# A second z unit behind the first, three groups in a row, and VectorE's half of the first rounding: a Mamba-2 and differential-attention trunk in fp32

## The chip, the cores and the metric

The kernel runs on one core of one Trainium2 chip. The metric is the device time of one execution in microseconds. The matrix unit (TensorE, PE in the profile, with its weight loads shown apart as PEld), VectorE (DVE), ScalarE (ACT), GpSimd (POOL) and SyncE (SP, which here only issues DMAs) each work through a queue of their own in order, and wait for each other by semaphores.

## What is computed

Two layers over 512 tokens of width 1024, all in float32. The first is a Mamba-2 layer, the second a differential attention layer against one shared set of keys and values; a norm ends it. The change touches the first layer alone:

```python
def mamba2_layer(x, norm_g, w_in, conv_w, conv_b, dt_bias, a_log, d_skip, gate_norm_g, w_out):
    h = rms_norm(x, norm_g)
    zxbcdt = h @ w_in                                  # z 2048 | x 2048, B 1024, C 1024 | dt 32
    z = zxbcdt[..., :SSM_D_INNER]
    xbc = silu(causal_depthwise_conv(zxbcdt[..., 2048:6144], conv_w, conv_b))   # 4 taps
    dt = softplus(zxbcdt[..., 6144:] + dt_bias)
    y = ssd_chunked_scan(xs * dt[..., None], -exp(a_log) * dt, bm, cm) + d_skip * xs
    y = gated_group_rms_norm(y, z, gate_norm_g)        # y * silu(z), normed in 8 groups of 256
    return x + y @ w_out
```

There are 8 groups of 4 heads; a group has its own B and C (128 wide each) and 256 columns of x.

## The kernel before

Each float32 product is made of three: both factors are split into a rounded half (`hi`) and a remainder (`lo`), and `mm3` issues hi by hi, hi by lo and lo by hi as 128x512 products. For a weight ScalarE makes `whi` from `raw`, with the norm's gain in it, and VectorE makes `wlo`; for the input the halves are `a_hi` and `a_lo` (`hh` and `hl` in the code, `split_x`).

The first layer is a row of units, `order_a`. A unit `z`*j* makes 512 columns of z (96 products of 128x512 in four banks `pz`, then Silu on ScalarE into `zs`, in halves of 256; group g needs `zt[g]`, so z*j* is for groups 2j and 2j+1). A unit `g`*i* makes B, C and x of one group (96 products in four banks `pg`), each bank followed by the convolution: VectorE multiplies the bank by the norm's row (`pg<-pg,ar_row`), ScalarE does the last tap and the bias (`xc<-pg`), VectorE the other three taps (`xc`, three instructions), ScalarE the Silu. A unit `o`*j* is a quarter of the output projection (`po`). Each unit fetches two blocks of weights, of 1 MB each, two blocks ahead (`segs`, `use`, `fetch`), through two `raw` buffers and three of `whi` and `wlo`. `TURNS` says in which order a unit takes its banks and its two blocks: kind 0 takes one block for all four banks and then the other, kind 1 both blocks for each of the first two banks.

Between these products the scan of each group (`ssd`) is fed in, piece by piece. A piece's place is in `PLACES`: so many blocks of three products after the group's own unit. `cb` makes C by B in a bank `pcb`; `bt` and `xt` transpose B and x (`pbt`, `pxt`), after which VectorE makes `xdt` and `dx`, POOL `xe`, and VectorE multiplies the decays `dec` by `pcb`; `st` makes the states (`psA`, `psB`, `hst`) and the products within a chunk (`pyd`, one half in a `long` bank); `o1` and `o2` make the parts from the states (`po1`, `po2`), VectorE scales them (`tmp`), POOL adds them, VectorE multiplies by z (`dx<-dx,zs`), ScalarE squares and sums, and VectorE makes the root of the norm in ten small steps (`v`, `y_i`, `y_y`, `y_c`); ScalarE scales by it (`tmp<-dx,y_y`); `y0` transposes the result (`pyt`), from which `yh` and `yl` are made for the output projection. There is one `long` bank; it holds `pcb` of a group, then half of `pyd`.

Ahead of all this stand z0 (its first block straight as the input lands), the norm of the input (`scales`: the root on VectorE, a diagonal `adiag`, and a product that spreads it over the partitions, `aps_r`), and the chain from `ps_dt` to the decays: about twenty instructions on VectorE, a transposition `ps_tt` at the place `tt`, a round trip through memory (`acs_d`, then `dec`), and per group eight POOL instructions and one exponential.

TensorE follows the program's order (`T.on`), so the table of places fixes its queue. VectorE's and ScalarE's queues in this layer are set by the scheduler of the tile framework, which puts weight halves ahead (`high_priority`) and fits the rest around them. Rows of the profile carry L70 where an engine is called through the helper `Ordered`.

Of the kernel before, what the change touches and what calls it, by code (L numbers as in the profile page):

```python
# [9 lines left out]
F32 = mybir.dt.float32  # L10
# [3 lines left out]
ALU = mybir.AluOpType  # L14
# [3 lines left out]
P = 128  # L18
S = 512
D = 1024  # L20
NT = S // P
# [16 lines left out]


PLACES = {  # L40
# [7 lines left out]
    "y2": (None,) * 7 + (72,),  # L48
}

# [28 lines left out]
def trunk(ctx, tc, x, x_t, par, w_dt, w_in, w_out, w_kvqg, w_bo, d_skip, lam_qk, fin_g, out):  # L79
    nc = tc.nc  # L80
    V, A, T = (Ordered(tc, e) for e in (nc.vector, nc.scalar, nc.tensor))
    GP = nc.gpsimd
# [4 lines left out]
    small = ctx.enter_context(tc.tile_pool(name="small", bufs=2))  # L87
# [13 lines left out]
    def long_bank(name):  # L101
        return psum.tile([P, 512], F32, tag="long", name=name)
# [1 line left out]

    order_a = "z0 g0 g1 z1 g2 g3 z2 g4 o0 g5 z3 g6 g7 o1 o2 o3".split()
    segs = []
    for it in order_a + ORDER_B:
        segs += [(it[0], int(it[1]) if len(it) == 2 else it, k) for k in range(2 if it[0] in "zgov" else 1)]  # L110
# [3 lines left out]
    nc.scalar.dma_start(prm[:], par[:, 0:C_CB])  # L114
    prc = const.tile([P, N_PAR - C_CB], F32, name="prc")
    x_tok = res.tile([P, NT, D], F32, name="x_tok")
    ident = const.tile([P, P], F32, name="ident")
    make_identity(nc, ident)
    sg1 = const.tile([P, 1], F32, name="sg1")
# [147 lines left out]
    def rsqrt(v, n, tag, bufs=2):  # L267


        y = small.tile([P, n], F32, tag=f"{tag}_y", name=f"{tag}_y", bufs=bufs)  # L270
        c = small.tile([P, n], F32, tag=f"{tag}_c", name=f"{tag}_c", bufs=bufs)
        iy = small.tile([P, n], I32, tag=f"{tag}_i", name=f"{tag}_i", bufs=bufs)

        def vyy():
            if n == 1:
                V.scalar_tensor_tensor(out=c, in0=y, scalar=v, in1=y, op0=ALU.mult, op1=ALU.mult)
            else:
                V.tensor_tensor(out=c, in0=y, in1=v, op=ALU.mult)
                V.tensor_tensor(out=c, in0=c, in1=y, op=ALU.mult)

        V.tensor_scalar(out=iy, in0=v.bitcast(I32), scalar1=1, scalar2=None, op0=ALU.logical_shift_right)
        V.tensor_scalar(out=y.bitcast(I32), in0=iy, scalar1=-1.0, scalar2=float(0x5F3759DF - 2 ** 31), op0=ALU.mult, op1=ALU.add)
        vyy()
        V.scalar_tensor_tensor(out=c, in0=c, scalar=-10.0 / 3.0, in1=c, op0=ALU.add, op1=ALU.mult)
        V.scalar_tensor_tensor(out=y, in0=c, scalar=5.0, in1=y, op0=ALU.add, op1=ALU.mult)
        vyy()
        root_end[0] = V.scalar_tensor_tensor(out=y, in0=c, scalar=-64.0 / 3.0, in1=y, op0=ALU.add, op1=ALU.mult)
        return y
# [39 lines left out]
    def scales(tag, ss):  # L328

        V.tensor_scalar(out=ss, in0=ss, scalar1=ROOT2 / D, scalar2=ROOT2 * EPS, op0=ALU.mult, op1=ALU.add)  # L330
        col = const.tile([P, NT], F32, tag="r_col", name=f"{tag}r_col")
        V.tensor_copy(col, rsqrt(ss, NT, "y"))
        w = small.tile([P, NT + 1, P], F32, tag="wide", name=f"{tag}diag", bufs=2)
        GP.memset(w[:, NT], 1.0)
        for t in range(NT):
            GP.tensor_tensor(out=w[:, t], in0=ident, in1=col[:, t:t + 1].to_broadcast([P, P]), op=ALU.mult)
        ps = long_bank(f"{tag}ps_r")
        T.on = True
        T.matmul(ps, lhsT=w[:, NT], rhs=w[:, 0:NT].rearrange("p t n -> p (t n)"), start=True, stop=True)
        T.on = False  # L340
        row = res.tile([P, S], F32, tag="r_row", name=f"{tag}r_row")
        A.copy(row, ps)
        return col, row
# [14 lines left out]
    def new_h(tag):  # L358
        return [res.tile([P, KD, S], F32R, tag=f"hT_{i}", name=f"{tag}_{i}") for i in ("hi", "lo")]
# [9 lines left out]
    hh, hl = new_h("a")  # L369
# [4 lines left out]
    bp2 = bctx.enter_context(tc.tile_pool(name="bp2", bufs=2))  # L374

    zt = {}
    yT = {}
    conv_out = {}

    def z_out(j, t, ps):  # L380

        for i in range(2):
            zs = bp2.tile([P, 256], F32, tag="zs", name=f"zs{j}_{t}_{i}", bufs=12)
            A.activation(zs, ps[:, i * 256:(i + 1) * 256], AF.Silu, scale=r_col[:, t:t + 1])
            zt[2 * j + i, t] = zs

    warm = ss_bank("warm")
    for i in range(17):  # L390
        T.transpose(warm[:, 0:P], ident, ident)
    xt = [bp2.tile([P, 2, S], F32, tag="yl", name=f"xt{i}", bufs=4) for i in range(4)]

    def split_x(k, n=slice(0, S)):
        A.copy(hh[:, k, n], xt[k // 2][:, k % 2, n])
        V.tensor_tensor(out=hl[:, k, n], in0=xt[k // 2][:, k % 2, n], in1=hh[:, k, n].bitcast(F32), op=ALU.subtract)


# [4 lines left out]
    wh, wl = ready.pop(("z", 0, 0))  # L403
    pz0 = [mm_bank(f"pz0_{t}") for t in range(NT)]
    V.on = A.on = True
    for k in range(4):
        lay(first[k])
        for n in (slice(0, 256), slice(256, S)) if k < 2 else (slice(0, S),):
            split_x(k, n)
    V.on = A.on = False  # L410
    for k in range(4):
        for t in range(NT):
# [2 lines left out]
    for k in range(4, KD):  # L415
        split_x(k)
# [3 lines left out]
    ss = bss[:, 1]  # L420
# [13 lines left out]
    for k in range(KD):  # L434
        for c in range(NQ):
            T.matmul(ps_dt[c * H:(c + 1) * H, 0:P], lhsT=dtw_raw[:, k, :], rhs=xt[k // 2][:, k % 2, c * P:(c + 1) * P],
                     start=k == 0, stop=k == KD - 1)
# [49 lines left out]
    def turned():  # L487
        yield "tt"
        ps_tt = ss_bank("ps_tt")
        for i, src in enumerate((dtp, acs, toe)):  # L490
            T.transpose(ps_tt[:, i * P:(i + 1) * P], src, ident)
        V.tensor_copy(tok[:, 0:3].rearrange("p a c h -> p (a c h)"), ps_tt[:, 0:3 * P])
        A.activation(tok[:, 3], tok[:, 1], AF.Exp)
        decays((0, 1))

    def runs_of(kind=1):

        at = {}
        for i, b, n in TURNS[kind]:
            k = at.get((i, b), 0)  # L500
            at[i, b] = k + n
            yield i, b, range(k, k + n)

    def z_proj(j):
        pz, w = {}, {}
        for t, b, ks in runs_of():
            if b not in w:
                w[b] = use(("z", j, b))
            if t not in pz:
                pz[t] = mm_bank(f"pz{j}_{t}")  # L510
            yield from tok_mm(pz[t], t, b, w[b], ks)
            if b and ks[-1] == 3:
                z_out(j, t, pz[t])
# [17 lines left out]
    def group_proj(g):  # L531
        fts = [(16 + g, "b", 1), (24 + g, "c", 2), (2 * g, "x0", 1), (2 * g + 1, "x1", 1)]
        pg, w, outs = {}, {}, []
        for i, b, ks in runs_of(min(g, 1)):
            if b not in w:
                w[b] = use(("g", g, b))
            if i not in pg:
                pg[i] = mm_bank(f"pg{g}_{i}")
            wh, wl = w[b]
            cs = slice(i * P, (i + 1) * P)  # L540
            for k in ks:
                kk = 4 * b + k
                mm3(pg[i], (wh[:, k, cs], wl[:, k, cs]), (hh[:, kk, :], hl[:, kk, :]), kk == 0, kk == KD - 1)
                yield
            if b and ks[-1] == 3:
                outs.append(conv(pg[i], *fts[i]))
        conv_out[g] = outs
# [26 lines left out]
    def resume(n, at, gen, places):  # L574
        kind = next(gen, None)
        if kind is not None:
            due.append((at + places[kind], len(due), at, gen, places))
# [19 lines left out]
    decs = {}  # L597
# [20 lines left out]
    def ssd(g):  # L618
        bc, cc, x0, x1 = conv_out.pop(g)
        xc = (x0, x1)  # L620
        dec, een, _ = decs.pop(g)
        hs = slice(R * g, R * g + R)

        yield "cb"
# [8 lines left out]
        bt = bp.tile([P, 3, P], F32, tag="bt", name=f"bt{g}")  # L633
# [4 lines left out]
        for j in range(2):  # L638
# [6 lines left out]
            with tc.issue_after(next_b.ins) if next_b else ExitStack():  # L645
                V.tensor_tensor(out=xdt[:, :, 2 * j:2 * j + 2, :], in0=pv, in1=dt_tok[:, :, h2].unsqueeze(3).to_broadcast([P, NQ, 2, HD]), op=ALU.mult)
                V.tensor_tensor(out=dx[:, :, 2 * j:2 * j + 2, :], in0=pv,
                                in1=dsk[:, h2].unsqueeze(1).unsqueeze(3).to_broadcast([P, NQ, 2, HD]), op=ALU.mult)
        xe = bp.tile([P, 3, R, HD], F32, tag="xe", name=f"xe{g}")
        for c in range(3):  # L650
            GP.tensor_tensor(out=xe[:, c], in0=xdt[:, c], in1=toe_tok[:, c, hs].unsqueeze(2).to_broadcast([P, R, HD]), op=ALU.mult)  # L651
        for h in range(R):
            V.tensor_tensor(out=dec[:, h], in0=dec[:, h], in1=pcb.rearrange("p (c l) -> p c l", l=P), op=ALU.mult)

# [36 lines left out]
        for c in (2, 3):  # L691
            T.matmul(po2[:, (c - 2) * 256:(c - 1) * 256], lhsT=cc[:, c * P:(c + 1) * P], rhs=hsf[:, c - 1], start=True, stop=True)
        V.tensor_tensor(out=tmp[:, 1], in0=po1[:, 256:512].rearrange("p (h e) -> p h e", e=HD),
                        in1=eacs_tok[:, 1, hs].unsqueeze(2).to_broadcast([P, R, HD]), op=ALU.mult)
        V.tensor_tensor(out=tmp[:, 2:4], in0=po2.rearrange("p (c h e) -> p c h e", h=R, e=HD),
                        in1=eacs_tok[:, 2:4, hs].unsqueeze(3).to_broadcast([P, 2, R, HD]), op=ALU.mult)
# [15 lines left out]
        yh = bp2.tile([P, 2, S], F32R, tag="yh", name=f"yh{g}", bufs=4)  # L712
# [3 lines left out]
        n = 2 if g == G - 1 else NQ  # L716
# [8 lines left out]
        yT[g] = (yh, yl)  # L725

    T.on = True
    resume(0, 0, turned(), {"tt": 22})
    first_layer()
    T.on = False  # L730

    hh, hl = new_h("b")
# [126 lines left out]
    st = {}  # L859
# [283 lines left out]
    y, f, o, dst = half(3, 0)  # L1143
# [8 lines left out]
    y, f, o, dst = half(3, 1)  # L1152
# [68 lines left out]
```

## Time and profile before

| | |
|---|---|
| median of 3 runs | 706.07 us (706.02 to 706.21) |
| the profiled execution | 707.18 us, of which 705.4 us span |
| PE busy | 696.1 us, 3838 matmul rows |
| DVE busy | 524.2 us |
| ACT busy | 426.3 us |
| POOL busy | 116.1 us |
| granted TensorE clock, mean | 0.998 |

The span goes from the first to the last instruction; the rest of an execution's time lies around it. A row of the chain or of a timeline begins with the start in us from the span's start and the length in us; xN counts merged instructions. What stands in square brackets is the idle time before it on its engine and what ended that. A row of the waits has the total in us, the count, and the longest. A plain float32 product shows as two rows, a transposition as one.

### The profile page before, as it was taken

To read this page: it belongs to the slowest core of one execution; us is meant where nothing else is said; L and a number is where in the kernel's file an instruction comes from. 1 tells how busy PE (TensorE), PEld (TensorE's weight loads), DVE (VectorE), ACT (ScalarE), POOL (GpSimd) and SP (SyncE) were. 2 spreads that over 40 slices of the span, in tenths; PEclk is the share of its full clock that TensorE was granted. 3 is DMA by queue.
4 is the path that set the end of the run, shared out by engine and by line. 5 is a ranking of instruction groups with operands and counts; after the bars stand their busy time and mean duration, and the time that the engine had idled before them with its cause. 6 is when DMAs were issued, how large, how long until landed. Compare 5 with 4: busy or idle time off the path is not lost.

```text
span 705.4 us, 10468 instructions
## 1 busy us (share of the span) xinstructions
PE 696.1 (99%) x3838; PEld 580.7 (82%) x3838; DVE 524.2 (74%) x1181; ACT 426.3 (60%) x931; POOL 116.1 (16%) x158
## 2 busy tenths in 40 slices
PE   8999999999999999999999999999999999999996
PEld 7888788888878888888888888888888888888884
DVE  5499967799489679569995757557778757787776
ACT  6859663573654547536635258567777667665546
POOL 0008242502406025042110101000000000000002
PEclk9999999999999999999999999999999999999999
DMA  8654314214125323313222111513112221130103
GB/s 293 257 193 170 120 60 135 105 61 179 42 79 180 105 76 120 110 70 120 64 84 94 60 60 53 194 60 113 67 60 77 80 83 61 60 106 14 31 1 119
DMA packets 13491, 70.85 MB, mean 100 GB/s; under 512 B 1792, under 2 KB 3328, under 8 KB 6016
## 3 DMA queue, kind: packets, MB, share of 16 engines
q1 hardware_dynamic: 13008, 69.90, 27.6%
q8 instruction: 30, 0.49, 0.3%
q10 hardware_dynamic: 432, 0.28, 0.1%
q14 instruction: 21, 0.17, 0.1%
HBM read 68.02 MB, written 2.16 MB: 99 GB/s over the span
## 4 chain that ended last, share of the span: by engine, by line
PE 78%; DVE 8%; ACT 5%; DMA 4%; issue 3%; POOL 2%; SPq 0%; ACTq 0%; POOLq 0%; DVEq 0%
PE po L70 16%; PE pg L70 14%; PE pt L70 8%; PE pq L70 6%; PE pk L70 6%; PE pv L70 6%; PE pz L70 6%; PE pb L70 3%; DMA raw<-in_w_in 3%; PE sc L70 3%; DVE wlo L70 2%; ACT whi L70 2%; PE pc L70 2%; PE pyd L70 2%; DVE xc L70 1%
## 5 line engine op out<-in xcount | busy, mean ns | idle before, releaser
L70 DVE SCALAR_TENSOR_TENSOR wlo<-raw,prm,whi 128x512 fp32r<-128x512 f32 (+1 forms) x240 | 149.3, 672 | 54.0 <-ACT whi L70 53.7
L70 ACT ACTIVATE whi<-raw,prm 128x512 fp32r<-128x512 f32 (+1 forms) x240 | 133.2, 629 | 46.7 <-PE pg L70 12.0
L70 PE MATMUL pg<-a_hi,whi 128*128 128x512 f32 x256 | 102.8, 402 | 0.0
L70 PE MATMUL pg<-a_hi,wlo 128*128 128x512 f32 x256 | 99.9, 390 | 0.0
L70 PE MATMUL pg<-a_lo,whi 128*128 128x512 f32 x256 | 99.7, 389 | 0.0
L70 DVE SCALAR_TENSOR_TENSOR xc<-pg,prc,xc 128x511 f32<-128x511 f32 (+2 forms) x96 | 70.9, 743 | 12.3 <-ACT xc L70 11.2
L70 PEld LDWEIGHTS pg<-a_hi,wlo 128*128 128x128 f32 x256 | 48.1, 188 | 10.3
L70 PEld LDWEIGHTS pg<-a_hi,whi 128*128 128x128 f32 x256 | 48.2, 188 | 9.6 <-ACT zs L70 0.2
L70 PEld LDWEIGHTS pg<-a_lo,whi 128*128 128x128 f32 x256 | 48.1, 188 | 9.4
L70 PE MATMUL po<-whi,yh 128*128 128x512 f32 x128 | 51.2, 400 | 0.0
L70 PE MATMUL pz<-whi,a_hi 128*128 128x512 f32 x128 | 49.7, 397 | 0.3 <-ACT a_hi L70 0.3
L70 PE MATMUL po<-whi,yl 128*128 128x512 f32 x128 | 49.9, 390 | 0.0
L70 PE MATMUL po<-wlo,yh 128*128 128x512 f32 x128 | 49.9, 390 | 0.0
L70 PE MATMUL pz<-whi,a_lo 128*128 128x512 f32 x128 | 48.9, 390 | 0.0
L70 PE MATMUL pz<-wlo,a_hi 128*128 128x512 f32 x128 | 48.9, 389 | 0.0
L1026 POOL TENSOR_TENSOR ot<-x_tok,fg 128x512 f32<-128x512 f32 x4 | 5.0, 1284 | 246.8 <-DVE x_tok L70 246.8
L70 ACT ACTIVATE xc<-xc 128x512 f32<-128x512 f32 x32 | 20.2, 630 | 40.5 <-DVE xc L70 36.7
L70 ACT ACTIVATE xc<-pg,prc 128x512 f32<-128x512 f32 x32 | 24.8, 774 | 28.3 <-DVE pg L70 27.9
L70 DVE CUSTOM_DVE_ANT_0 s<-sc,bias 128x128 f32<-128x128 f32 (+3 forms) x64 | 29.4, 488 | 16.0 <-PE sc L70 15.5
L70 ACT ACTIVATE s<-s,mx 128x128 f32<-128x128 f32 (+3 forms) x64 | 35.6, 557 | 9.1 <-DVE mx L70 8.9
L651 POOL TENSOR_TENSOR xe<-xdt,tok 128x256 f32<-128x256 f32 x24 | 14.0, 613 | 159.3 <-DVE xdt L70 159.3
L70 ACT ACTIVATE tmp<-dx 128x256 f32<-128x256 f32 x32 | 13.1, 410 | 36.8 <-DVE dx L70 36.8
(237 smaller groups left out, 1651.1 us busy)
## 6 DMA issues: line engine op xcount, KB each, us to landing
raw<-in_w_in SPq DMA_DIRECT2D x22, 1024.0 KB, 4.9
raw<-in_w_kvqg SPq DMA_DIRECT2D x16, 1024.0 KB, 4.8
dec<-acs_d SPq DMA_DIRECT2D x8, 1024.0 KB, 5.1
raw<-in_w_out SPq DMA_DIRECT2D x8, 1024.0 KB, 4.9
raw<-in_w_bo SPq DMA_DIRECT2D x4, 1024.0 KB, 4.8
x_tok<-in_x SPq DMA_DIRECT2D x4, 512.0 KB, 9.0
out<-ot SPq DMA_DIRECT2D x6, 256.0 KB, 2.1
raw<-in_w_in SPq DMA_DIRECT2D x4, 256.0 KB, 4.9
```

Source lines behind the costliest of these rows:

```text
L70: i = op(*args, **kw)
L651: GP.tensor_tensor(out=xe[:, c], in0=xdt[:, c], in1=toe_tok[:, c, hs].unsqueeze(2).to_broadcast([P, R, HD]), op=ALU.mult)
L1026: GP.tensor_tensor(out=o, in0=y, in1=f, op=ALU.mult)
```

## The change

- `order_a` becomes z0 z1 g0 g1 g2 z2 g3 g4 ... where it was z0 g0 g1 z1 g2 g3 z2 g4 ...; from g4 on the units are the same. `PLACES` has new numbers for groups 0 to 3 (and small ones for the last `y0`), and `tt` moves from 22 to 36. z1 now takes the first kind of turns, and g0 the second.
- z1's second halves go to a tile of the `yh` ring, `spare`, where they took four of the twelve `zs` buffers.
- VectorE rounds the first 256 columns of the input's first block, which ScalarE did.
- TensorE's warm-up is ten float32 products over a blank tile that VectorE clears, where it was 17 transpositions of the identity that POOL makes.
- The diagonal for the norm's row is one VectorE product straight from the root, ahead of the copy of the column, where it was four POOL products behind it.

```diff
 PLACES = {
...
-    "y0": (61, 85, 76, 99, 89, 85, 69, 69),
+    "y0": (70, 79, 99, 79, 89, 87, 69, 70),
...
-    order_a = "z0 g0 g1 z1 g2 g3 z2 g4 o0 g5 z3 g6 g7 o1 o2 o3".split()
+    order_a = "z0 z1 g0 g1 g2 z2 g3 g4 o0 g5 z3 g6 g7 o1 o2 o3".split()
...
+    blank = small.tile([P, D], F32, tag="wide", name="blank", bufs=2)[:, 0:P]
+    V.memset(blank, 0.0)
...
-        V.tensor_copy(col, rsqrt(ss, NT, "y"))
+        root = rsqrt(ss, NT, "y")
         w = small.tile([P, NT + 1, P], F32, tag="wide", name=f"{tag}diag", bufs=2)
         GP.memset(w[:, NT], 1.0)
-        for t in range(NT):
-            GP.tensor_tensor(out=w[:, t], in0=ident, in1=col[:, t:t + 1].to_broadcast([P, P]), op=ALU.mult)
+        V.tensor_tensor(out=w[:, 0:NT], in0=ident.unsqueeze(1).to_broadcast([P, NT, P]),
+                        in1=root.unsqueeze(2).to_broadcast([P, NT, P]), op=ALU.mult)
+        V.tensor_copy(col, root)
...
-            zs = bp2.tile([P, 256], F32, tag="zs", name=f"zs{j}_{t}_{i}", bufs=12)
+            if (j, i) == (1, 1):
+                if not t:
+                    spare.append(bp2.tile([P, 2, S], F32, tag="yh", name="spare", bufs=4))
+                zs = spare[0][:, t // 2, t % 2 * 256:t % 2 * 256 + 256]
+            else:
+                zs = bp2.tile([P, 256], F32, tag="zs", name=f"zs{j}_{t}_{i}", bufs=12)
...
-    for i in range(17):
-        T.transpose(warm[:, 0:P], ident, ident)
+    for i in range(10):
+        T.matmul(warm[:, 0:P], lhsT=blank, rhs=blank, start=True, stop=True)
...
+    V.tensor_copy(hh[:, 0, 0:256], xt[0][:, 0, 0:256])
     for k in range(4):
         lay(first[k])
         for n in (slice(0, 256), slice(256, S)) if k < 2 else (slice(0, S),):
-            split_x(k, n)
+            split_x(k, n, (k, n.start) == (0, 0))
...
     def z_proj(j):
         pz, w = {}, {}
-        for t, b, ks in runs_of():
+        for t, b, ks in runs_of(min(j - 1, 1)):
...
-        for i, b, ks in runs_of(min(g, 1)):
+        for i, b, ks in runs_of():
...
-        dec, een, _ = decs.pop(g)
...
+        dec, een, _ = decs.pop(g)
         for h in range(R):
...
-    resume(0, 0, turned(), {"tt": 22})
+    resume(0, 0, turned(), {"tt": 36})
```

What this moves shows in three places. The first is VectorE's queue at the root of group 0's norm (`v40` to the last `y_y`, from the squares `ss40`). Before, it reads:

```order
L70 SCALAR_TENSOR_TENSOR xc3_896<-pg1_3_765,prc_72,xc3_896 128x511
L70 TENSOR_SCALAR v40_871<-ss40_796 128x4
L70 SCALAR_TENSOR_TENSOR xc3_896<-pg1_3_765,prc_72,xc3_896 128x510
L70 TENSOR_SCALAR y_i_875<-v40_871 128x4
L70 SCALAR_TENSOR_TENSOR xc3_896<-pg1_3_765,prc_72,xc3_896 128x509
L70 TENSOR_SCALAR y_y_873<-y_i_875 128x4
L70 TENSOR_TENSOR y_c_874<-y_y_873,v40_871 128x4
```

Now (`xc4` and `xc5` are group 2's x, `wlo12` a weight block of g3):

```order
L70 TENSOR_SCALAR v40_1090<-ss40_1000 128x4
L70 TENSOR_TENSOR pg2_3_1138<-pg2_3_1138,ar_row_252 128x512
L70 SCALAR_TENSOR_TENSOR xc4_1171<-pg2_2_1125,prc_72,xc4_1171 128x511
L70 SCALAR_TENSOR_TENSOR wlo12_1224<-raw12_1221,prm_70,whi12_1223 128x512 x2
L70 TENSOR_SCALAR y_i_1094<-v40_1090 128x4
L70 SCALAR_TENSOR_TENSOR wlo12_1224<-raw12_1221,prm_70,whi12_1223 128x512 x2
L70 SCALAR_TENSOR_TENSOR xc4_1171<-pg2_2_1125,prc_72,xc4_1171 128x510
L70 SCALAR_TENSOR_TENSOR xc5_1214<-pg2_3_1138,prc_72,xc5_1214 128x511
L70 TENSOR_SCALAR y_y_1092<-y_i_1094 128x4
L70 SCALAR_TENSOR_TENSOR xc4_1171<-pg2_2_1125,prc_72,xc4_1171 128x509
L70 SCALAR_TENSOR_TENSOR xc5_1214<-pg2_3_1138,prc_72,xc5_1214 128x510
L70 TENSOR_TENSOR y_c_1093<-y_y_1092,v40_1090 128x4
```

Between `v40` and the last step stood two convolution taps; now eleven 512-wide instructions stand there (one more `xc5` follows these rows).

The second place is TensorE's queue at group 0's transposes. Before, they stand in z1, ahead of `pbt1`:

```order
L70 MATMUL pz1_3_1003<-whi7_654,a_lo_81 128x512
L70 MATMUL pyt0_0_891<-ident_74,tmp0_797 128x128 x4
L70 MATMUL pyt0_1_892<-ident_74,tmp0_797 128x128 x4
L70 MATMUL pbt1_1047<-ident_74,xc17_676 128x128 x3
L70 MATMUL pz1_3_1003<-whi7_654,a_hi_80 128x512
```

Now they stand in z2, right ahead of group 1's states:

```order
L70 MATMUL pz2_0_1233<-whi11_972,a_lo_83 128x512
L70 MATMUL pyt0_0_1110<-ident_76,tmp0_1001 128x128 x4
L70 MATMUL pyt0_1_1111<-ident_76,tmp0_1001 128x128 x4
L70 MATMUL pz2_0_1233<-whi11_972,a_hi_82 128x512
L70 MATMUL pz2_0_1233<-wlo11_973,a_hi_82 128x512
L70 MATMUL pz2_0_1233<-whi11_972,a_lo_83 128x512
L70 MATMUL psA1_1210<-xe1_1201,bt1_1152 128x256 x2
L70 MATMUL psB1_1284<-xe1_1201,bt1_1152 128x256
L70 MATMUL pyd1_1_1291<-xdt1_1154,dec1_608 64x64 x16
```

From the end of `pcb1` to `pyt0` the queue now holds 72 products of 128x512; from `po20` on it is 72 as well, since `po10` and `po20` come right behind `pcb1`.

The third is TensorE's queue around group 3's products within a chunk. Before, `pyd3` comes in g4 and `pcb4` only after it, behind `po23`:

```order
L70 MATMUL psA3_1948<-xe3_1939,bt3_1877 128x256 x2
L70 MATMUL psB3_1995<-xe3_1939,bt3_1877 128x256
L70 MATMUL pyd3_1_2002<-xdt3_1879,dec3_1236 64x64 x16
L70 MATMUL pyd3_0_2001<-xdt3_1879,dec3_1236 64x64 x16
L70 MATMUL po13_2077<-hst3_1947,xc27_1457 128x256
```

Now, in o0:

```order
L70 MATMUL po0_0_1_2015<-whi16_1752,yl0_1109 128x512
L70 MATMUL pcb4_2019<-xc28_1874,xc20_1837 128x128 x4
L70 MATMUL po0_0_1_2015<-whi16_1752,yh0_1108 128x512
L70 MATMUL po0_0_1_2015<-wlo16_1753,yh0_1108 128x512
L70 MATMUL po0_0_1_2015<-whi16_1752,yl0_1109 128x512
L70 MATMUL po0_0_1_2015<-whi16_1752,yh1_1428 128x512
L70 MATMUL po0_0_1_2015<-wlo16_1753,yh1_1428 128x512
L70 MATMUL po0_0_1_2015<-whi16_1752,yl1_1429 128x512
L70 MATMUL psA3_1966<-xe3_1957,bt3_1908 128x256 x2
L70 MATMUL psB3_2035<-xe3_1957,bt3_1908 128x256
L70 MATMUL pyd3_1_2042<-xdt3_1910,dec3_1345 64x64 x16
```

`pcb4` and `pyd3_1` both take the `long` bank, and their order is turned round.

More of the change, by code (lines that the diff above doesn't have):

```diff
@@ L376, in trunk @@
     zt = {}
+    spare = []
     yT = {}
@@ L389, in trunk, with split_x @@
     warm = ss_bank("warm")
-    for i in range(17):
-        T.transpose(warm[:, 0:P], ident, ident)
+    for i in range(10):
+        T.matmul(warm[:, 0:P], lhsT=blank, rhs=blank, start=True, stop=True)
     xt = [bp2.tile([P, 2, S], F32, tag="yl", name=f"xt{i}", bufs=4) for i in range(4)]
-    def split_x(k, n=slice(0, S)):
-        A.copy(hh[:, k, n], xt[k // 2][:, k % 2, n])
+    def split_x(k, n=slice(0, S), laid=False):
+        if not laid:
+            A.copy(hh[:, k, n], xt[k // 2][:, k % 2, n])
         V.tensor_tensor(out=hl[:, k, n], in0=xt[k // 2][:, k % 2, n], in1=hh[:, k, n].bitcast(F32), op=ALU.subtract)
```

12 rows, old and new, of the table PLACES are left out of this document.

## The prediction

> **What bounds the kernel now.** I read the page's busy table and chain first, then the list of who waited for whom, then the chain in order of time, then the timelines of VectorE (DVE), ScalarE (ACT) and TensorE (PE) around the first layer's groups.
>
> ```profile
> span 705.4 us, 10468 instructions
> PE 696.1 (99%) x3838; PEld 580.7 (82%) x3838; DVE 524.2 (74%) x1181; ACT 426.3 (60%) x931; POOL 116.1 (16%) x158
> PE 78%; DVE 8%; ACT 5%; DMA 4%; issue 3%; POOL 2%; SPq 0%; ACTq 0%; POOLq 0%; DVEq 0%
> PE warm L70 <- POOL ident masks.py:199: 1.5, 1, 1.5
> PE psA L70 <- POOL xe L651: 0.4, 1, 0.4
> PE pz L70 <- ACT a_hi L70: 0.3, 1, 0.3
> PE pyt L70 <- ACT tmp L70: 0.3, 1, 0.3
> PEld pyt L70 <- ACT tmp L70: 1.4, 4, 0.6
> ```
>
> TensorE is busy 99% of the span, and its whole list of waits is four short ones: before the first product, at group 0's states (`psA`), and at one group's transposes (`pyt`, the matmuls' list and the weight loads' list tell of the same place). So an order of work that leaves the products alone can win back at most these waits, two or three microseconds, while every wait that it makes lands on the span in full. What decides is whether VectorE and ScalarE still deliver ahead of TensorE in the new order. VectorE is the close one:
>
> ```profile
> 60.00:80.00 20.00, 19.55 (x150) 15.83 (x149) 18.59 (x29) 14.91 (x18) 11.55 (x15) 1.00 0.19 56
> 120.00:140.00 20.00, 20.00 (x135) 16.77 (x131) 16.66 (x26) 9.24 (x17) 11.82 (x14) 1.00 0.29 106
> ```
>
> These are two stretches of 20 us; behind the length stand the busy times of PE, weight loads, DVE, ACT and POOL, then the granted clock. VectorE is busy 18.59 and 16.66 us of 20 while TensorE hardly waits.
>
> **The change, part by part.** *Front.* The first products wait for both the rounded weights and the rounded input:
>
> ```profile
> 1.47 3.89 PE L70 MATMUL warm<-ident 128*128 128x128 f32 x17 [1.47 <-POOL ident masks.py:199]
> 4.54 0.72 ACT L70 ACTIVATE whi<-raw,prm 128x512 fp32r<-128x512 f32 x1 [1.86 <-DMA prm<-in_par]
> 5.27 0.69 ACT L70 CAST a_hi<-xt 128x256 fp32r<-128x256 f32 x2
> 5.71 1.43 PE L70 MATMUL pz<-whi,a_hi 128*128 128x512 f32 x4 [0.35 <-ACT a_hi L70]
> ```
>
> With VectorE rounding the first half beside ScalarE's 0.72 us, the products can start about when `whi` ends (5.26 + 0.09 = 5.35 instead of 5.71): 0.36 at most, 0 if the input's half lands only then. I take 0.25. The ten blank products are two passes each, 20 x about 0.21 us = 4.3, and need only a memset, so they end before 5.35 if they start by 1.0, a little after the pool's own memsets; otherwise they cost part of the 0.25. The diagonal for the norm's row moves from four POOL products to one on VectorE, and the copy of the column behind it; TensorE didn't wait there (no such row in its list), so I cost it at nothing; uncovered it would be the one instruction, 0.6.
>
> *The z unit moved ahead.* z1 has the same 96 products wherever it stands; its weights are loads 2 and 3 on SP's queue, as g0's were. The chain that makes `dt` and the decays gets these 96 products, 21.8 us, as more cover, so `tt` at 36 costs nothing. On SP's queue the four `acs_d` writes and two `dec` reads now stand behind load 7 where they stood behind load 6; `dec0` is needed after `pcb0`, 126 products or 28.6 us behind `ps_tt`. ScalarE gets four more table loads:
>
> ```profile
> L70 ACT ACT_TABLE_LOAD x23 | 29.5, 1283 | 4.6 <-DVE xc L70 3.1 <-PEq L1214 1.2
> ```
>
> 1.28 us each, 5.1 together, beside z1, whose 21.8 us leave ScalarE only the Silu of z and some weight halves: nothing, and 1.28 where a bank of z1 were released that much late. That z1 takes its weights half by half and g0 row by row, that z1's second halves lie in a `yh` buffer (`spare`, one of four, free again ahead of group 4), and that `decs` is read later in the code add no instruction. Group 0's wait at `psA` goes, since its transposes stand 22 us behind its last product. So does group 2's at `pyt`. Prices:
>
> ```profile
> 74.39 1.27 PE psA L70 x4
> 75.66 0.57 PE psB L70 x2
> 81.21 1.29 PE po L70 x6
> 84.57 0.89 PE pcb L70 x8
> 85.46 18.38 PE pz L70 x81
> 103.84 0.87 PE pyt L70 x8
> 104.72 0.33 PE pbt L70 x3
> 118.21 0.86 PE psA L70 x4
> 119.07 0.43 PE psB L70 x2
> ```
>
> Group 0's `psA` and `psB` took 1.27 + 0.57, group 1's without a wait 0.86 + 0.43: 0.55, and about 0.5 of waiting ahead of them, 1.05 together. Group 2's transposes:
>
> ```profile
> 173.24 1.46 PE L70 MATMUL po<-hst,xc 128*128 128x256 f32 x6
> 195.24 1.71 ACT L70 ACTIVATE tmp<-dx,y_y 128x256 f32<-128x256 f32 x4
> 195.80 1.96 PE L70 MATMUL pyt<-ident,tmp 128*128 128x128 f32 x8 [0.35 <-ACT tmp L70]
> ```
>
> Eight transposes from first start to last end take 1.96 - 0.16 of pipeline instead of 0.87, so 0.9, and 0.5 before them: 1.4. One more pair of `po1` and `po2` stands together: 0.2. Gains: 0.25 + 1.05 + 1.4 + 0.2 = 2.9 us.
>
> *The new wait at group 0's transposes.* By the order, TensorE has this between the end of `pcb1` and `pyt0`: three `po` products (1.29), 72 products of 128x512 (18.38 / 81 = 0.227 each, 16.3), `pbt1` (0.33), eight `pxt1` transposes (0.87 as for `pyt`), and some 0.2 of changes between kinds: 19.0 us. VectorE has, from `dec1` (which waits for `pcb1`) to the last instruction of group 0's root: 4 `dec`, 2 `tmp`, 3 `pg`, 12 `xc`, 8 `wlo`, 3 `dx` by `zs`, 2 `xdt`, 10 small ones. Their rows:
>
> ```profile
> 45.68 2.72 DVE L70 SCALAR_TENSOR_TENSOR wlo<-raw,prm,whi 128x512 fp32r<-128x512 f32 x4
> 53.34 0.69 DVE L70 TENSOR_TENSOR pg<-pg,ar_row 128x512 f32<-128x512 f32 x1
> 53.93 2.28 DVE L70 SCALAR_TENSOR_TENSOR xc<-pg,prc,xc 128x510 f32<-128x510 f32 x3
> 56.13 0.69 DVE L70 TENSOR_TENSOR pg<-pg,ar_row 128x512 f32<-128x512 f32 x1
> 64.77 2.47 DVE L70 TENSOR_TENSOR dec<-dec,pcb 128x512 f32<-128x512 f32 x4
> 71.77 0.68 DVE L70 TENSOR_TENSOR xdt<-pxt,tok 128x512 f32<-128x512 f32 x1
> 115.04 2.32 DVE L70 SCALAR_TENSOR_TENSOR xc<-pg,prc,xc 128x511 f32<-128x511 f32 x3 [0.85 <-ACT xc L70]
> 122.30 0.41 DVE L70 TENSOR_TENSOR tmp<-po,tok 128x256 f32<-128x256 f32 x1
> 122.63 0.41 DVE L70 TENSOR_TENSOR dx<-dx,zs 128x256 f32<-128x256 f32 x1
> 190.48 0.16 DVE L70 TENSOR_SCALAR v<-ss 128x4 f32<-128x4 f32 x1
> 191.87 0.17 DVE L70 TENSOR_TENSOR y_c<-y_y,v 128x4 f32<-128x4 f32 x1
> ```
>
> From start to start (rows overlap by 0.08): `wlo` 0.68, `pg` 0.59, `xc` (56.13 - 53.93) / 3 = 0.73, 512-wide products 0.6, 256-wide ones 0.33, the root's small steps (191.87 - 190.48) / 7 = 0.2. Sum: 4 x 0.6 + 0.33 + 0.6 + 3 x 0.59 + 12 x 0.73 + 8 x 0.68 + 3 x 0.33 + 2 x 0.6 + 10 x 0.2 = 23.5 us without a pause. It pauses: 0.85 where a convolution's first tap waits for ScalarE (row at 115.04; `xc26` stands right behind its `pg`), about 0.33 three times where `dx` by `zs` waits for POOL's additions, and about 2 at `xc18` and `wlo11`, whose ScalarE halves stand behind `dec2`'s exponential and two table loads. I take 4.0, so 27.5, and 0.5 for ScalarE's first scaling (1.71 for four): 28.0 against 19.0. TensorE waits 9.0 us at `pyt0` (5.0 with no pause; 12 with pauses of 7), and 0.9 more for the paced transposes as at 195.80. A check: group 2 of this trace took from the end of its `po` products, 173.24 + 1.46 = 174.7, to the scaling at 195.24, 20.5 us; in the new order TensorE needs 19.0 - 1.3 = 17.7 over the same stretch, so it would wait even at that pace. Queued behind the transposes on TensorE: all of z2, group 1's `psA` and `pyd`; nobody can overtake.
>
> *The clock after it.* The clock is granted in full until TensorE has been idle a while:
>
> ```profile
> 699.20:702.50 3.30, 0.00 (x0) 0.00 (x0) 2.57 (x9) 1.96 (x5) 0.00 (x0) 1.00 0.76 284
> 702.60:705.40 2.80, 0.00 (x0) 0.00 (x0) 0.00 (x0) 0.00 (x0) 0.00 (x0) 0.50 0.46 158
> ```
>
> The sixth figure falls from 1.00 to 0.50 some 3.4 us after the last product, which ended at 699.1. An idle stretch of 9 us will do that too. At the start it took from 1.47 until after the first product at 5.71 (the four of that row need 1.43 us) before the pace was full, some 4.8 us; 1 us of it is the paced transposes anyway, and half of the other 3.8 is lost: 1.9 us (0 to 3). [...]
>
> *A second new wait, at `pyd3`.* `pcb4` now stands ahead of `pyd3`, and both take the one `long` bank, so `pyd3_1` waits until VectorE has multiplied `dec4` by `pcb4`. From the first half of `pxt3` to there TensorE has 24 products (5.45), four `pxt3` transposes (0.43), `pyt2` (0.87), `pcb4` (0.89), `psA` and `psB` (1.29) and 0.4 of changes: 9.3 us. VectorE has 4 `xdt`/`dx` (2.4), one `pg` (0.6), 3 `xc` (2.2), 4 `wlo` (2.7), 2 `yl` (1.2), one `x_tok` (0.6) and 4 `dec` (2.4): 12.1. Wait: 2.8 us (0 if the first wait has let VectorE run ahead, 4.5 if it starts late). From group 4 on the order is as before.
>
> **Sum.** 9.0 + 0.9 + 1.9 + 2.8 - 2.9 = +11.7 us: a span of 717.1 against 705.4, and 718.9 for an execution like the profiled one (707.18). That one is 1.1 above the median of the runs, 706.07; to the median the sum gives 717.8.
>
> **Rivals.** *VectorE keeps up* (ends on the other side): the waits at `psA` and `pyt` go and no new one comes, 706.07 - 2.9 = 703.2. For it speaks that TensorE's list of waits is nearly empty though VectorE was busy 18.59 us of 20 already; against it that 23.5 us of queue would have to fit in 18.5. It decides at the point where group 0's root is done 18.5 us after `pcb1`. *A small wait*: VectorE never pauses, 5.0 + 0.9, about 1 for the clock, no second wait: +4.0, 710.1. For it: the busiest row above has 1.4 us of pause in 20. Against it: every convolution's first tap waits for ScalarE. *A large one*: pauses of 7 us (VectorE busy 16.66 of 20, as from 120 us on, would make 28.2 of 23.5, a pause of 4.7 already, and POOL's work or ScalarE's queue can add to it), 12 + 0.9 + 3 + 4.5 - 2.9 = +17.5, 723.6. *The change doesn't remove the two old waits*: +2.4 to the forecast, 720.2, inside its range.
>
> **How the numbers follow.** Forecast (waits at `pyt0` and `pyd3`, clock lost) 0.65, small wait 0.15, large 0.12, VectorE keeps up 0.06, the gains and a tiny wait cancel 0.02. Slower by over 0.2% (1.4 us, about what a measurement of this kernel can tell from no change) 0.92, within it 0.02, faster 0.06. Range: from just under the small wait, 709.5, to 722.0, which leaves out most of the large case and the fast one.
>
> **What would show it.** Right: in the new trace's list of waits PE `pyt` <- ACT `tmp` of 8 to 10 us, once, near 132 to 142 us; a stretch there with a granted clock under 1.00; a wait of some 3 us before `pyd` near 230 us on DVE `dec`; no wait at `psA` of group 0. Wrong: `pyt0` starting within 1 us of the product before it, or VectorE busy less than 20 of the 28 us up to it. My sum fails if VectorE's pauses are far from 4.0 us, or if ScalarE, not VectorE, ends last there.

## The result and the profile after

The changed kernel takes 722.76 us (median of four executions, 720.73 to 723.60) against 706.05 for the kernel before: a ratio of 1.0232, 95% interval 1.0211 to 1.0254, slower. The forecast was 717.8, with a range up to 722.0: the direction and the place were right, the size was 5 us short. Below are, from the page of after, the span and the busy line, and then the waits on TensorE that matter here (us in total, times, longest).

```profile
span 719.0 us, 10492 instructions
PE 697.8 (97%) x3841; PEld 582.5 (81%) x3841; DVE 524.0 (73%) x1184; ACT 432.8 (60%) x934; POOL 112.6 (16%) x154
```

```profile
PE pyt L70 <- ACT tmp L70: 8.9, 1, 8.9
PE pyd L70 <- issue: 3.8, 1, 3.8
PE pyt L70 <- DVE dx L70: 0.3, 1, 0.3
```

Both forecast waits are there and `psA` is gone from the list. TensorE's timeline and VectorE's show the second one:

```profile
219.13 1.04 PE L70 MATMUL pxt<-ident,xc 128*128 128x128 f32 x8
228.18 0.59 PE L70 MATMUL psB<-xe,bt 128*128 128x256 f32 x2
232.56 1.64 PE L70 MATMUL pyd<-xdt,dec 128*64 128x64 f32 x49 [3.79 <-issue]
219.92 0.74 DVE L70 SCALAR_TENSOR_TENSOR wlo<-raw,prm,whi 128x512 fp32r<-128x512 f32 x1
220.58 0.69 DVE L70 TENSOR_TENSOR xdt<-pxt,tok 128x512 f32<-128x512 f32 x1
229.98 2.48 DVE L70 TENSOR_TENSOR dec<-dec,pcb 128x512 f32<-128x512 f32 x4
```

`pyd3` starts 0.1 us behind the end of `dec4` by `pcb4` (229.98 + 2.48), though the list calls the wait "issue". From the start of `psB` to that of `pyd` it is 4.38 us, where group 1's take 0.53 (146.09 to 146.62): TensorE loses 3.9 us there, and I forecast 2.8. (The expectations below say 4.06, 0.2 more than this difference to group 1.) VectorE's work from `xdt3` to there took 232.46 - 220.58 = 11.9 us as forecast (12.1), but it began about 1 us after the first half of the transposes, behind a `pg` and a `wlo`; I had let it begin at once.

What sets the first wait stands in the chain of waits, in order of time (start, length, what), from the first step of group 0's root to ScalarE's scaling that `pyt0` waits for:

```profile
131.41 0.08 DVE v L70
131.49 0.60 DVE pg L70
132.09 0.65 DVE xc L70
132.74 1.72 DVE wlo L70 x2
134.46 0.08 DVE y_i L70
134.54 1.31 DVE wlo L70 x2
135.85 1.32 DVE xc L70 x2
137.17 0.08 DVE y_y L70
137.24 1.30 DVE xc L70 x2
...
140.22 0.17 DVE y_y L70
140.40 0.02 issue
140.42 1.72 ACT tmp L70 x4
```

VectorE has no pause here. But of the 9.0 us from 131.41 to 140.4 less than 2 are the root: its ten small steps stand one by one between group 2's convolution (`pg`, `xc`) and the next weights (`wlo`), which TensorE does not need for `pyt0`. TensorE's rows from there to group 1's states:

```profile
140.98 1.67 PE L70 MATMUL pyt<-ident,tmp 128*128 128x128 f32 x4 [8.94 <-ACT tmp L70]
...
146.09 0.59 PE L70 MATMUL psB<-xe,bt 128*128 128x256 f32 x2
```

The clock by windows (length; busy times of PE, weight loads, DVE, ACT, POOL; then the granted clock, the DMAs' share and GB/s; the boundaries are laid on the changes of the clock in this trace and on steps of 3.41 us from there):

```profile
131.65:135.06 3.41, 0.40 (x2) 0.00 (x0) 3.41 (x6) 2.08 (x4) 1.60 (x3) 1.00 0.71 288
135.06:138.47 3.41, 0.00 (x0) 0.00 (x0) 3.41 (x7) 0.48 (x1) 0.00 (x0) 0.50 0.41 115
141.89:145.30 3.41, 3.07 (x10) 2.30 (x11) 2.45 (x4) 1.41 (x3) 0.00 (x0) 0.50 0.02 5
227.22:230.63 3.41, 1.55 (x8) 1.00 (x6) 3.41 (x7) 0.37 (x1) 0.62 (x1) 1.00 0.72 255
230.63:234.05 3.42, 1.49 (x51) 1.52 (x53) 3.42 (x7) 0.63 (x1) 0.52 (x1) 1.00 0.15 58
```

Half clock from 135.06 to 145.30, 10.24 us, and none at the second wait. This execution, 720.73, is the lowest of the four and has a mean clock of .990; the other three, 2 to 3 us longer, have .986 and .987. Finding what they lost was the first experiment.

### The profile page after: what moved, and what is told of

Its sections match the earlier page's. It is cut to its first block, busy times and chain, and to the rows that moved or that the text cites. A ratio compares the mean times of both kernels' runs of the same rounds, so it can differ in the third digit from the quotient of the medians.

```text
span 719.0 us, 10492 instructions
## 1 busy us (share of the span) xinstructions
PE 697.8 (97%) x3841; PEld 582.5 (81%) x3841; DVE 524.0 (73%) x1184; ACT 432.8 (60%) x934; POOL 112.6 (16%) x154
## 3 DMA queue, kind: packets, MB, share of 16 engines
q1 hardware_dynamic: 13008, 69.90, 27.2%
## 4 chain that ended last, share of the span: by engine, by line
PE 88%; DMA 4%; DVE 4%; ACT 2%; issue 1%; POOL 1%; SPq 0%; ACTq 0%; POOLq 0%
PE pg L70 22%; PE po L70 16%; PE pz L70 9%; PE pt L70 7%; PE pq L70 6%; PE pv L70 6%; PE pk L70 6%; PE pb L70 3%; PE sc L70 3%; DMA raw<-in_w_in 2%; PE pyd L70 2%; PE pc L70 2%; PE pyt L70 1%; DVE wlo L70 1%; PE psA L70 1%
## 5 line engine op out<-in xcount | busy, mean ns | idle before, releaser
L70 ACT ACTIVATE whi<-raw,prm 128x512 fp32r<-128x512 f32 (+1 forms) x240 | 133.2, 629 | 44.4 <-PE po L70 12.1
L70 DVE SCALAR_TENSOR_TENSOR xc<-pg,prc,xc 128x511 f32<-128x511 f32 (+2 forms) x96 | 71.0, 746 | 15.2 <-ACT xc L70 14.2
```

What stands on the lines that cost most here:

```text
L70: i = op(*args, **kw)
```

## The experiments

**Where the other executions lose 2 to 3 us (e1).** The changed kernel again; no edit.

Expected of e1:

> The changed kernel once more, for the 2 to 3 us by which its timed runs (722.7 to 723.6) lie above its profiled one (720.73). Mean clocks of .987 against .990 make about 5 us more at half clock there. Theory A (a second fall): the wait of 4 us ahead of pyd3 lets the clock fall a second time in most executions, some 5 us at half clock from about 235 us on. Theory B (a longer first spell): one spell only, after pyt0, of about 15 us where the profiled one had 10.24. Theory C (not the clock): the same spell of 10 us and the time is lost elsewhere. Median 722.7 by all; in a profile of 722 or more, A shows two spells of half clock before 300 us, B one of 15 us, C one of 10 us.

Measured: 722.74 us (720.13 to 724.16). The profiled execution was the longest one, and its windows around `pyd3` read:

```profile
229.03:232.44 3.41, 0.67 (x4) 0.24 (x2) 3.41 (x7) 0.37 (x1) 0.62 (x1) 1.00 0.71 288
232.44:235.86 3.42, 2.37 (x44) 2.40 (x46) 3.38 (x7) 0.63 (x1) 0.62 (x1) 0.50 0.02 5
235.86:239.27 3.41, 3.41 (x30) 2.91 (x28) 2.49 (x5) 1.14 (x3) 0.00 (x0) 0.50 0.32 86
```

Theory A: the wait is the same, but here one window of 3.41 us holds most of it (TensorE busy 0.67), and the clock is at half for the next 6.83. In the first trace the same wait was cut in two by a boundary (busy 1.55 and 1.49), and nothing fell. The price, by the start of group 4's `psA` in after and in this run:

```profile
269.51 1.02 PE L70 MATMUL psA<-xe,bt 128*128 128x256 f32 x4
```

```profile
233.49 0.80 PE L70 MATMUL pyd<-xdt,dec 128*64 128x64 f32 x10 [3.79 <-issue]
273.04 1.02 PE L70 MATMUL psA<-xe,bt 128*128 128x256 f32 x4
```

39.55 us from `pyd3` to there against 36.95: 2.6 us. Of nine timed executions of this kernel two have a clock of .990 (720.13, 720.73); seven have .986 or .987 and a median of 722.81, 2.4 us more. Four of the runs below leave this wait as it is (e2, e5, e6, e8), and in all four profiles the clock falls behind it, for 3.41 us in e2 (mean clock .993) and 6.83 in the others (.989, .989 and .987); after is the only one of six where it does not.

**Filling the waits so that the clock stays (e2, e3).** Transposes of the identity into a bank that is overwritten, ahead of the waiting instruction; e3 has 28 more ahead of `pyd3`:

```diff
+            if (g, j, a) == (0, 0, 0):
+                for _ in range(72):
+                    T.transpose(pyt[0][:, 0:P], ident, ident)
```

Expected of e2:

> 72 transposes of the identity into the bank of pyt0, which only TensorE needs, directly ahead of group 0's transposes: 7.8 us of work (0.109 each) inside the wait of 8.9, so that TensorE never idles for more than about 1 us there while it still waits until the same moment for VectorE and ScalarE. The output is not changed by them. Only the clock's part of the loss can go. A: the first spell goes, about 1.4 us, the second stays: 721.3, mean clock .993. B: the whole of about 4 us goes: 718.7, mean clock .998. C: 720 to 722.7. If the transposes held anything up, slower than 722.7.

Expected of e3:

> As the run before, and 28 more transposes of the identity (3.1 us) into pyd3_0's bank ahead of pyd3, so that the second wait is filled too. A: the second spell goes as well, 2.6 us less than the run before: 718.7, clock .998. B: the same as the run before, 718.7. C: the same as the run before. VectorE is what both waits wait for, so the rest, about 12 us over the kernel before, stays by every theory.

Measured: 722.24 (721.51 to 724.68) and 722.08 (720.24 to 722.72): hardly a gain. A (721.3, then 718.7) and B (718.7) are missed; the times fit C (720 to 722.7, then the same), whose premise, a single spell, e1's trace refutes. In the first the clock still fell, for 3.41 us, behind a window in which the transposes paced by ScalarE left TensorE busy for 2.19 us of 3.42, and it fell at the second wait as well (mean clock .993).

```profile
140.36:143.78 3.42, 2.19 (x10) 1.42 (x11) 1.72 (x3) 2.47 (x6) 0.00 (x0) 1.00 0.00 0
143.78:147.19 3.41, 3.41 (x12) 2.23 (x13) 0.86 (x2) 0.74 (x2) 0.50 (x1) 0.50 0.00 0
```

In the second the 28 transposes had to wait for their own bank (PE `pyd` <- DVE `yl`, 1.7 us) and then ran past the moment when `dec4` was done. Both are inconclusive on the price; the next pair asks it again.

**The bank behind the second wait (e4)**, and the first spell's price on top of it (e9: 78 transposes ahead of the first of `pyt0`, and three ahead of each of the next three):

```diff
-    "cb": (14, 14, 14, 14, 5, 5, 14, 12),
+    "cb": (14, 14, 14, 14, 14, 5, 14, 12),
```

Expected of e4:

> One place changed: pcb4 at 14 instead of 5, behind pyd3, so that pyd3_1 no longer needs the bank that dec4 x pcb4 still reads. If that bank makes the second wait, the 4.06 us ahead of pyd3 go to 0 to 0.8. A: the second spell goes with it: 3.3 + 2.6 less, 716.8, mean clock .990 to .991. B: 3.3 less, 719.4, mean clock .987. If the wait is VectorE's backlog in general, it comes back at a later place and the time stays above 721.

Expected of e9:

> The price of the clock at pyt0 by itself: the kernel of e4 (pcb4 behind pyd3, 719.0 with a spell of 10.24 us at half clock) with 78 transposes of the identity ahead of group 0's first transpose and three ahead of each of the next three, into columns of pyt0's own bank that are written last, so that TensorE stays busy while it waits for the same instructions. If the clock costs what the spell shows, half of the 2.8 us of work that fell into it: 717.6, mean clock .996 or more. By my prediction's term, 1.9: 717.1. If the clock is hidden behind VectorE there: 719.0 at the higher clock.

Measured: 719.01 (717.63 to 719.30), 3.7 less, between A (716.8) and B (719.4): the 3.9 us at `pyd3` became 0.95 inside `pyd3` and 0.4 at `psB3`, so the one `long` bank made the second wait. That is 2.5 us of waiting; the 1.2 that are left are less than the 2.4 that I read above from the second fall. The profiled execution, 717.63, has the first spell alone (mean clock .992); the other three (.990), 1.1 to 1.7 us longer, were not profiled. Filled, the kernel took 717.15 (716.87 to 718.48) at a mean clock of .998 to .999, by the medians 1.9 less again, which is what I had put down for the first spell. The two profiled executions, 717.63 and 717.24, are only 0.4 apart, so this price differs from execution to execution.

**Queue, backlog or place?** In e5 VectorE's last taps for group 2 and the next small halves are held until the root is done:

```diff
-        V.tensor_tensor(out=u, in0=ps, in1=r_row, op=ALU.mult)
+        with tc.issue_after(root_end[0].ins) if ft in (4, 5) else ExitStack():
+            V.tensor_tensor(out=u, in0=ps, in1=r_row, op=ALU.mult)
```

with the same line ahead of the taps, and ahead of `rest(k)` for the thirteenth load.

Expected of e5:

> The changed kernel, with VectorE's last taps for group 2 (its features x0 and x1) and the small halves of the next weights held until group 0's root is done. In the changed kernel's trace the root's first step starts at 131.33 and its last ends at 140.38, ten steps of 0.16 us with 7.6 us of those other products among them; TensorE stands from 131.9 to 141.0. Theory Q (the order in VectorE's queue): together the steps take 1.8 us, the wait ahead of pyt0 falls from 8.9 to 1.5 to 2, the clock stays full there, some 2 us more are lost at pyt0's second bank because dx1 comes later, pyd3's wait stays: 722.7 - 7.2 + 2 - 1.9 = 715.6. Theory V (my prediction: VectorE's whole backlog): what is held back is missed just as long at the next place, psA1 or pyd1, and the time stays above 720.

Measured: 718.99 (718.67 to 719.72). VectorE's timeline: the root runs from 130.67 to 133.78 and ends 6.6 us earlier than in after:

```profile
130.67 0.16 DVE L70 TENSOR_SCALAR v<-ss 128x4 f32<-128x4 f32 x1
130.86 0.61 DVE L70 TENSOR_SCALAR y_i<-v 128x4 int32<-128x4 int32 x1
131.50 0.54 DVE L70 TENSOR_SCALAR y_y<-y_i 128x4 int32<-128x4 int32 x1
132.07 0.53 DVE L70 TENSOR_TENSOR y_c<-y_y,v 128x4 f32<-128x4 f32 x1
...
133.62 0.16 DVE L70 SCALAR_TENSOR_TENSOR y_y<-y_c,y_y 128x4 f32<-128x4 f32 x1
```

and TensorE's waits:

```profile
PE pyd L70 <- issue: 3.8, 1, 3.8
PE pyt L70 <- ACT tmp L70: 3.2, 1, 3.2
PE pyt L70 <- DVE dx L70: 2.4, 1, 2.4
```

8.9 became 3.2, and 2.4 came at the second bank. Q named this, 3.4 us too low in time: three of the steps took 0.5 to 0.6 us instead of 0.16, and the clock fell here after all, to 0.50 at 134.45, behind a window with TensorE busy for 0.22 us of 3.41. V, "above 720", fails by 1 us. Holding alone is worth 3.8 us.

Expected of e6:

> One place changed: group 0's transposes pyt0 at 80 instead of 70, ten places or 30 products of 0.227 us, 6.8 us, later. Theory P (they just stand too early): the wait falls from 8.9 to 2.1 and nothing takes its place: 722.7 - 6.8 - 0.9 - 1.9 = 713. Theories Q and V: psB1 and pyd1, now ahead of them, need group 1's hst1 and dx1 from VectorE, which stand behind the same root; a wait of 3 to 4 us comes back there, 1.8 more at pyt0's second bank, and the gain is 2.5 us of waiting and up to 2 of the clock: 718 to 720.

Measured: 720.17 (719.73 to 721.03). P is out: with `pyt0` 6.8 us later, most of the waiting only changes its place, as Q and V said; the time is 2.6 us less.

```profile
PE psB L70 <- DVE hst L70: 4.6, 1, 4.6
PE pyd L70 <- issue: 4.2, 1, 4.2
PE pyt L70 <- DVE yl L70: 1.7, 1, 1.7
```

Then both together (e10): `x0`'s taps held behind the root, `x1`'s and the weights' behind `dx1`, and six places, the five below

```diff
-    "st": (39, 39, 63, ...   "o1", "o2": (46, 46, ...   "y0": (70, 79, 99, ...
+    "st": (39, 44, 63, ...   "o1", "o2": (46, 52, ...   "y0": (80, 79, 97, ...
```

and `pcb4` at 14. In e11 stand the six places alone; e16 is e10 with `pcb2` at 22.

Expected of e10:

> Both waits aimed at together: VectorE's taps of group 2's feature x0 held until group 0's root is done, those of x1 and the next weights' small halves until dx1 is done; pcb4 at 14; group 1's st, o1, o2 at 44, 52, 52; y0 of group 0 at 80 and of group 2 at 97. Theory Q (order in VectorE's queue and places, not VectorE's sum of work): 1 to 2 us of waiting stay, no half clock before the end: 722.7 - (9.1 + 1.8 + 1.9 + 4.05 + 2.6) + 1.5 = 704.8, a little below the kernel before. Theory V (VectorE's backlog): what is held back is missed later, at least 5 us of waiting stay: 709 or more.

Expected of e11:

> The places of e10 without holding anything back on VectorE. Theory Q: hst1 still stands behind group 2's taps and the steps of the root among them, so 3 to 4 us of waiting come at psB1, with 0 to 2 for the clock: 708 to 710. Theory P (places alone): as e10, 705.

Expected of e16:

> The kernel of e10 with pcb2 at 22 instead of 14, behind the moment when dx1 has read pyd1_1 from the one long bank. e10 had 1.7 us of waiting there, 1.2 ahead of po2 of group 1, 0.6 at psB1 and 0.4 at psB3. Theory Q: the 1.7 go, the others stay or shrink: 708.8 - 1.7 = 707.1, or 706 with the 1.2 at po2 gone too. Theory V: the wait moves on as large: 708.8. Faster than the kernel before (705.8) by neither.

Measured: 708.77 (708.24 to 709.64), 710.70 (710.00 to 710.85) and 707.67 (707.07 to 708.35). Behind the warm-up the first has three waits, the longer two:

```profile
PE pcb L70 <- DVE dx L70: 1.5, 1, 1.5
PE po L70 <- DVE yl L70: 1.0, 1, 1.0
```

That is 4 us above Q's number and just under V's bound of 709, so it does not decide. The longest waits behind the warm-up in the second and in the third:

```profile
PE psB L70 <- DVE hst L70: 3.3, 1, 3.3
```

```profile
PE pyt L70 <- DVE dx L70: 1.5, 1, 1.5
```

The third decides: with the same group order and the same work on VectorE it took away 15.1 of the 16.7 us. So with these places and holds the order of z1 and three groups costs 1.6 us by the medians (ratio 1.0017, interval 1.0007 to 1.0028, against the kernel before). The rest was places, one bank and the order in VectorE's queue. Taken one upon the other, the six places (`pcb4` among them) were worth 12.1 us, the holding 1.9 more (710.70 - 708.77), and `pcb2` 1.1.

**Front (e7) and order (e8) apart.**

Expected of e7:

> The kernel before with the change's edits at the front alone: ten products of a blank tile in place of 17 transposes, VectorE rounds the input's first half, one product on VectorE makes the norm's diagonal; order and places as before (z1 behind g1, tt at 22). My terms: 0.25 less, 0.6 more at most for the diagonal: 705.5 to 706.5. A rival: the diagonal and the cast push VectorE's chain to dt back while z1's 21.8 us of cover are not there, and TensorE waits up to 3 us at ps_tt: 707 to 709.

Expected of e8:

> The changed kernel with the front of before (17 transposes, ScalarE rounds the whole input, POOL makes the diagonal): order, places, turns and the spare tile as changed. If order and places make all of the loss: 722.5 to 723.2, the same waits at pyt0 (9) and pyd3 (4). If part of the loss belongs to the front: below 721.

Measured: order alone 722.66 (722.48 to 723.95), the same as both. The front alone on the kernel before 711.00 (708.66 to 711.19), ratio 1.0064 (1.0051 to 1.0077): slower by 5, worse than the rival. Its waits, in the execution of 708.66:

```profile
PE ps_tt L70 <- DVE pre L70: 1.6, 1, 1.6
PE ps_tt L70 <- DVE e L70: 1.0, 1, 1.0
```

The other five have clocks of .994 to .997 against its .998. The moved z1, with `tt` at 36, hides this in the changed kernel; without that cover my "nothing" for the front costs 3 us of waits, and 2 more in most executions, where the lower clocks point to a spell like those above, not profiled.

**Are the old waits in each execution?** e12 is the kernel before with one place changed, `y0` of group 2 at 80 for 76; e13 to e15 are the kernel before itself.

Expected of e12:

> The kernel before with one place changed, group 2's transposes at 80 instead of 76. The 1.4 us that I counted at these transposes (0.5 ahead of the first, 0.9 of pacing) are gone if they only stood four places too early: 704.4. If VectorE's work behind them makes the same wait elsewhere: 705.8.

Expected of e13:

> The kernel before, profiled again, to see whether the waits that I counted as gains are there in each execution. Theory M (they come and go): an execution at the median, 705.8, has one or none of them, and the gains of the change against the median are about 1 us less than I counted. Theory N (they are in each): 0.6 us ahead of psA0 and 1.4 at pyt2 in every profile, and 705.8 differs from 707.2 elsewhere.

Expected of e14:

> A second execution of the kernel before. Theory M: the waits at psA0 and pyt2 differ from those of the run before and follow the time. Theory N: the same 0.6 and 1.4 us.

Expected of e15:

> A third execution of the kernel before. Theory M: the waits at psA0 and pyt2 differ between the three and follow the time. Theory N: the same 0.6 and 1.4 us in all three.

Measured: 705.95 (705.14 to 707.08), ratio 0.9996 (0.9987 to 1.0005): no gain, where 704.4 was expected. The three further executions took 706.05, 706.04 and 707.61. Group 2's transposes in them, in that order (1.96 in the profile of the prediction):

```profile
195.39 1.24 PE L70 MATMUL pyt<-ident,tmp 128*128 128x128 f32 x8
```

```profile
195.54 1.07 PE L70 MATMUL pyt<-ident,tmp 128*128 128x128 f32 x8
```

```profile
196.14 1.96 PE L70 MATMUL pyt<-ident,tmp 128*128 128x128 f32 x8
```

Theory M for `pyt2`: at 706.05 the transposes are not paced and nothing waits ahead of them; at 707.2 and 707.6 they are. The 0.6 us ahead of `psA0` is there in three of the four profiles (not at 707.61). The 707.61 are not `pyt2`'s alone: there `ps_dt` begins at 30.82 already, against 28.68 in the first of the three.

## Why the prediction was wrong in size and right in kind

- *The first place as a whole*: 9.0 + 0.9 + 1.9 = 11.8 forecast, 11.9 measured in after: 14.2 us from the end of the last product before `pyt0` (131.66 + 0.23) to `psB` at 146.09, less about 2.35 for eight transposes, three products and `psA` at full pace (0.80, 0.69 and 0.86 from start to start at 222.77, 224.34 and 227.32). The same stretch of e1 gives 12.8. The three parts came out less well than their sum, so the sum is in part luck.
- *The wait at `pyt0`*: 9.0 forecast, 8.9 by the list and 9.1 from start to start. Right, and by the right count, since the queue's order was given: VectorE took 27.2 us from `dec` by `pcb1` (113.15) to the end of the root, 27.5 forecast. My reading of it, that VectorE had that much to do first, was too wide: in e5 the root is done in 3.1 us, and in e11 VectorE, with nothing held back, is in time for most of the later places.
- *Paced transposes*: 0.9 forecast; 0.9, and 0.7 more at the second bank, which waits for `dx1`. Short by 0.7.
- *The clock after it*: 1.9 forecast; of the 11.9 in after 1.2 are left for it, of the 12.8 in e1 1.9, and 1.9 lie between the medians of e4 and e9.
- *The wait at `pyd3`*: 2.8 forecast, 3.9 measured; I let VectorE start at once. Short by 1.1.
- *The clock after that*: not in the sum, which has the clock for the first wait alone and gives no reason why the second should not cost it. It falls in most executions (seven of nine by their clocks, five of six by profiles), and costs 2.4 to 2.6 us; e4 bears out at least 1.2 of it. This is the largest step missed.
- *Gains*: 2.9 forecast. Between the two profiled executions 11.9 + 3.9 = 15.8 us of losses stand against a difference of 13.55, so some 2.2 came. And 1.4 of the forecast gains, at `pyt2`, are not in a median execution of the kernel before: the profiled one is 1.1 above the median, and I took that wait off the median all the same.
- *Front*: 0.25 forecast; order alone and the whole change are the same to 0.1 us, so none that can be seen. That it costs nothing held only because z1 covers it (e7).

The miss of 5.0 is made up of three parts. The profiled executions differ by 13.55 where the sum has 11.7: 1.9, of which 1.1 is the wait at `pyd3` and 0.7 the gains. The median of after lies 2.0 above its profiled execution, where the clock did not fall a second time. The median of before lies 1.1 below its profiled execution. Why the last 0.7 of the gains did not come is open. Of the rivals the large one, 723.6, came nearest in time, by other terms: its first wait of 12 us did not come.

## What to carry to other kernels

Where one engine is late, look whether the steps that are waited for are long or only stand one by one between others: the chain in order of time shows it. Either remedy alone, holding the others back (3.8 us) or moving the waiting instruction (2.6), let the waiting come back elsewhere; the places of all the pieces together gave most of it back. Price every wait with the clock that it may cost, and where its cost differs from execution to execution, as behind `pyd3` (2.6 us or nothing), take the likelier case, not none. Before a wait of the profiled execution is counted as a gain, ask whether a median execution has it.

## What the runs showed of the hardware

The granted clock changed on a grid of 3.413 us: in after at 135.06, 145.30 and 715.33, 10.24 and 570.03 us apart, which is 3 and 167 times that; in e1 at 136.87 and 232.44, 95.57 us apart, 28 times. The phase was not the same: after 135.06 the next step of after's grid is 138.47, and e1's change at 136.87 lies between. The prediction speaks of idle time; the clock also fell to 0.50 behind windows that were far from idle: with TensorE busy for 0.67 us of 3.41 in e1 and for 2.19, of paced transposes, in e2. It did not fall behind 1.55 and 1.49 in after. It came back to full behind a window busy for 3.07 (after); behind 2.31 and 2.37 (e1) it stayed at half. The first three windows at half in e1, and the one before them:

```profile
133.46:136.87 3.41, 0.00 (x0) 0.00 (x0) 3.41 (x7) 0.34 (x1) 0.00 (x0) 1.00 0.27 113
136.87:140.28 3.41, 0.00 (x0) 0.00 (x0) 3.25 (x11) 1.26 (x2) 0.00 (x0) 0.50 0.92 308
140.28:143.70 3.42, 2.31 (x7) 1.39 (x8) 1.63 (x4) 2.29 (x5) 0.00 (x0) 0.50 0.00 0
143.70:147.11 3.41, 3.41 (x11) 2.76 (x10) 1.11 (x2) 0.59 (x1) 0.00 (x0) 0.50 0.02 5
```

No busy time sorts all of these: the clock fell behind 2.19 and not behind 1.49. The same wait of 3.9 us cost nothing more in after, where a boundary cut it in two, and 2.6 us more in e1.

VectorE's small steps of 0.16 us took 0.53 to 0.61 us in e5 while GpSimd's `xe` ran (130.83 to 132.58), and 0.16 right after it:

```profile
130.83 1.75 POOL L665 TENSOR_TENSOR xe<-xdt,tok 128x256 f32<-128x256 f32 x3 [9.07 <-DVE v L70]
```

No run tested the cause.
